# Two transformer blocks on one core: low-order keys beside zeros in 128-row tiles, and value products over 128 columns

## The chip, the cores and the metric

The program runs on one core of one Trainium2 chip. The metric is device time in microseconds of one execution, start to end; of the kernel before there are three timed runs and one further execution that was profiled.

## The reference, cut to what matters

Two transformer blocks run one after the other on a sequence of 1024 tokens of width 1024. The first block holds a differential attention (4 heads, each with two score maps over 64 columns and values 128 wide), a stick-breaking attention (8 heads of 64), a cross attention and an MLP. The second block holds a sliding-window attention (8 query heads over 2 key and value heads of 64, window 128), an RWKV mixer and a gated linear attention (GLA). The change touches three of them:

```python
# differential attention: per head, two maps c over 64 columns each
s = einsum('bhcqd,bhckd->bhcqk', qblk, kh) * scale
p = softmax(where(mask, s, -inf)); w = p[:, :, 0] - lam * p[:, :, 1]
o = einsum('bhqk,bhkv->bhqv', w, vh)
# stick breaking: 8 heads of 64
z = einsum('bhqd,bhkd->bhqk', qblk, kh) * scale
a = exp(where(strict, log_beta + between, -inf)); o = einsum('bhqk,bhkd->bhqd', a, vh)
# sliding window: 8 query heads, 2 key/value heads, blocks of 128
s = einsum('bnqhgd,bnkhd->bnhgqk', qb, kb) * (D ** -0.5) - slopes * dist
p = softmax(concat([where(valid, s, -inf), sink]))[..., :-1]
o = einsum('bnhgqk,bnkhd->bnqhgd', p, vb)      # then gated by silu of another projection
```

## The kernel before, in words

**Precision.** Every large product is done with operands split in two: a high part in float32r and a low part that holds the rest. A projection adds three products (`mm3`, lines 206 to 210: high by high, high by low, low by high). In the attentions the two parts share one tile: `stack_q` (line 434) puts the high part of a head's 64 query rows in one half of the 128 partitions and the low part in the other; `stack_k` (446) puts the high part of the head's keys in both halves of a tile `ks`, so one product over 128 rows gives high by high plus low by high. The low parts of both heads' keys go into one tile `kl`, head 0 in partitions 0 to 63 and head 1 in 64 to 127. The third product is then taken over the 64 rows of one head: line 467 in `scores`, line 1675 in the window attention. On TensorE every score tile is thus a product over 128 rows (466, 1674) followed by one over 64 rows into the same accumulator.

**Values.** In the stick-breaking attention (`sb_units`, 524) the values of a pair of heads lie side by side as 128 columns. Step c of a unit (line 552) multiplies one head's 64 columns into the 64 output partitions of that head (559); both heads of a query block share one PSUM tile, and after head 1 ScalarE copies the whole tile out (564). In the window attention step `pv` (1712) multiplies 64 value columns of group g into 64 partitions (1718); after group 1 VectorE multiplies the tile by the gate (1722). The differential attention has values of 128 columns already (697).

**Order of the work.** The first stage (`mix`, 755) goes through four pairs of stick-breaking heads and then four differential heads. For each, a list of units (query block i, head h) has steps: a (scores and the elementwise chain), b (transposes, 480, copied out at 482), c (value product), and for the differential heads every fourth unit d. `g_units` (725) runs step a of unit k, then b of unit k-2, then c of unit k-4 (lags `LAG`, set at line 801). `weave` (142) fills in projection matmuls of the heads to come between the steps, in proportion to costs written out by hand: `(a, 107 * n), (b, 109 * n), (c, 130 * n)` at line 569, and ratios at lines 814 and 816. Each engine then works through its own queue in order. The stick-breaking chain of step a is: ScalarE sigmoid (539), GpSimd mask (540), VectorE scan (544) and difference (547); then TensorE transposes (480). That of the differential attention: VectorE maximum (663), ScalarE exponential (673), VectorE weighting (684).

The window attention (`w_units`, 1652) runs twice, for tokens 0 to 511 (c = 0) and 512 to 1023 (c = 1), with 8 units each (4 query blocks b by 2 groups g) and lags 0, 2 and 3. Its fill is projection work of the second block. In step `tr` of group 1 the gate rows `sg` are fetched by a DMA on SyncE's queue (1698 to 1702), into a scratch tile of the ring "t2" (5 buffers).

**Memory.** Rings of buffers per tag stand in `BUFS` (187): `kl` has 4 buffers, `wv` 5. Weight pieces go round `wh` (8) and `wv` (`wpiece`, 278): eight pieces hold one set of weights. The rotary step of the differential projection (`g_df_proj`, 609) has four small tiles of its own (627).

Of the kernel before, what the change touches and what calls it, by code (L numbers as in the profile page):

```python
# [22 lines left out]
P = 128  # L23
# [145 lines left out]
class K:  # L169
# [11 lines left out]
    def nm(s, p):  # L181
# [2 lines left out]


    BUFS = {
        "act": 4, "qs": 8, "ks": 8, "kl": 4, "wv": 5, "stg": 3, "pw": 5, "tr": 5, "t2": 5, "v": 3, "u": 1, "wh": 8, "ad": 3, "wt4": 8, 
    }

    def tl(s, pool, shape, tag, dt=F32):  # L190
# [73 lines left out]
    def consts_b(s):  # L264
        nc, A = s.nc, s.A
        c = s.cst
        s.ident = c.tile([P, P], F32, name="ident")
        s.nc.sync.dma_start(s.ident, A["c_id"])
        s.identb = c.tile([P, P], BF16, name="identb")
        nc.vector.tensor_copy(s.identb, s.ident)  # L270
        zb = c.tile([P, P], BF16, name="zb")
        nc.vector.memset(zb, 0.0)
        s.causb = c.tile([P, P], BF16, name="causb")
        nc.gpsimd.affine_select(
            s.causb, zb, pattern=[[-1, P]], compare_op=ALU.is_ge, fill=NEG, base=0, channel_multiplier=1
        )
# [167 lines left out]
        return out  # L444

    def stack_k(s, pool, src, dst=None):
        nc = s.nc
        kl = s.tl(pool, [P, CH], "kl", F32R) if dst is None else dst[2]
        out = []
        for h in range(2):  # L450
            k = s.tl(pool, [P, CH], "ks", F32R) if dst is None else dst[h]
            a, b = slice(64 * h, 64 * h + 64), slice(64 - 64 * h, 128 - 64 * h)
            nc.scalar.activation(k[a], src[a], AF.Copy)
            nc.scalar.activation(k[b], src[a], AF.Copy)
            nc.vector.tensor_tensor(kl[a], src[a], k[a].bitcast(F32), ALU.subtract)
            out.append(k)
        return out + [kl]

    def scores(s, qs, ks, h, i, w0, w1, diag):

        mm = s.nc.tensor.matmul
        c, n = w0 // CH, w1 - w0
        ps = s.ps()
        a = slice(64 * h, 64 * h + 64)
        q = qs[i // 4][h][:, (i % 4) * P : (i % 4 + 1) * P]
        mm(ps[:, :n], q, ks[c][h][:, :n], start=True, stop=False)
        mm(ps[:, :n], q[a], ks[c][2][a, :n], start=False, stop=not diag)
        if diag:
            mm(ps[:, n - P : n], s.identb, s.causb, start=False, stop=True)
        return ps[:, :n]  # L470
# [53 lines left out]
    def sb_units(s, p, res, v):  # L524
        nc = s.nc
        V = nc.vector
        st = {}

        def unit(i, h):
            w = (i + 1) * P  # L530
            u = {}

            def a():
                m = u["m"] = s.tl(s.wk, [P, T + 1], "pw")
                nc.gpsimd.memset(m[:, w : w + 1], 1.0)
                for w0 in range(0, w, CH):
                    w1 = min(w, w0 + CH)
                    ps = s.scores(res["q"], res["k"], h, i, w0, w1, False)
                    nc.scalar.activation(m[:, w0:w1], ps, AF.Sigmoid, scale=s.r18n[:, i : i + 1])
                nc.gpsimd.affine_select(  # L540
                    m[:, w - P : w], m[:, w - P : w], pattern=[[-1, P]], compare_op=ALU.is_gt, fill=1.0,
                    base=0, channel_multiplier=1,
                )
                V.tensor_tensor_scan(  # L544
                    m[:, :w][:, ::-1], m[:, :w][:, ::-1], s.zero.to_broadcast([P, w]), 1.0, ALU.mult, ALU.add
                )
                V.tensor_tensor(m[:, :w], m[:, 1 : w + 1], m[:, :w], ALU.subtract)

            def b():
                u["t"] = s.transposed(u["m"], i + 1)  # L550

            def c():
                if h == 0:
                    st["po"] = s.ps()
                    if i % 4 == 0:
                        st["y"] = s.tl(s.wk, [P, CH], "t2")
                po, y = st["po"], st["y"]
                for j in range(i + 1):
                    nc.tensor.matmul(
                        po[64 * h : 64 * h + 64, :P], v[:, j, 64 * h : 64 * h + 64], u["t"][j],  # L560
                        start=j == 0, stop=j == i,
                    )
                if h == 1:
                    nc.scalar.activation(y[:, (i % 4) * P : (i % 4 + 1) * P], po[:, :P], AF.Copy)
                    if i % 4 == 3:
                        s.put_y(4 + p, i // 4, y)
# [42 lines left out]
    def g_df_proj(s, at, w, res):  # L609
        nc = s.nc  # L610
        V = nc.vector
        wh, wl = w
        for c in range(2):
            u = s.tl(at, [P, 4, 256], "u")
            for b in range(4):
                blk = c * 4 + b
                ps = s.ps()
                yield from s.g_proj_T(blk, wh, wl, 256, ps[:, :256])
                while b == 0 and s.pend:
                    yield from s.pend.pop(0)()  # L620
                nc.scalar.activation(u[:, b, :], ps[:, :256], AF.Copy, scale=s.r1[:, blk : blk + 1])
            uv = u.rearrange("p b (c d) -> p b c d", d=64)
            x1, x2 = uv[:, :, :, 0:8], uv[:, :, :, 8:16]
            sh = [P, 4, 4, 8]
            co = s.cos[:, c * 4 : c * 4 + 4, None, :].to_broadcast(sh)
            si = s.sin[:, c * 4 : c * 4 + 4, None, :].to_broadcast(sh)
            t = [s.sm.tile(sh, F32, tag=f"rt{z}", name=s.nm("rt"), bufs=1) for z in range(4)]
            V.tensor_tensor(t[0], x1, co, ALU.mult)
            V.tensor_tensor(t[1], x2, si, ALU.mult)
            V.tensor_tensor(t[2], x2, co, ALU.mult)  # L630
            V.tensor_tensor(t[3], x1, si, ALU.mult)
            V.tensor_tensor(x1, t[0], t[1], ALU.subtract)
# [960 lines left out]
    def win_load(s, mx, c):  # L1593
# [4 lines left out]
        kst = [mx.tile([P, P + CH], F32R, name=s.nm("k2")) for _ in range(3)]  # L1598
# [53 lines left out]
    def w_units(s, wn, c, qst, kst, bias, sink, one):  # L1652
# [6 lines left out]
        def unit(b, g):  # L1659
# [7 lines left out]
            def a():  # L1667
                p = u["p"] = wn.tile([P, 4, 2 * P], F32, tag="wp", name=s.nm("wp"), bufs=3)
                t = s.sm.tile([P, 6, 4], F32, tag="wt", name=s.nm("wt"))
                for z in range(2):  # L1670
                    ps = s.ps([P, 2, 2 * P])
                    for y in range(2):
                        q = qst[2 * z + y][g][:, (b % 4) * P : (b % 4 + 1) * P]
                        mm(ps[:, y, :w], q, kst[g][:, k0 : k0 + w], start=True, stop=False)  # L1674
                        mm(ps[:, y, :w], q[ga], kst[2][ga, k0 : k0 + w], start=False, stop=True)  # L1675
# [19 lines left out]

            def tr():
                u["t"] = []
                if g == 1:
                    sg = st[("sg", b)] = s.tl(s.wk, [P, 4, P], "t2")
                    s.nc.sync.dma_start(  # L1700
                        sg, s.pd[0:512, b * P : (b + 1) * P].rearrange("(h p) t -> p h t", p=P)
# [8 lines left out]
                    u["t"].append(t)  # L1710

            def pv():
                if g == 0:
                    st["po"] = s.ps()
                po = st["po"]
                for z in range(nk):
                    v = s.vt[:, b - nk + 1 + z, 256 + 64 * g : 320 + 64 * g]
                    mm(po[ga, :], v, u["t"][z], start=z == 0, stop=z == nk - 1)  # L1718
                if g == 1:
                    sg = st.pop(("sg", b))  # L1720
                    y = s.tl(s.wk, [P, 4, P], "t2")
                    V.scalar_tensor_tensor(
                        y, po.rearrange("p (h t) -> p h t", t=P), 0.5, sg, ALU.mult, ALU.mult
                    )
# [681 lines left out]
```

## Time and profile before

| | |
|---|---|
| timed runs | 2459.67, 2461.28, 2468.86 us; median 2461.28 |
| profiled execution | 2454.21 us, its span 2452.0 us |
| granted TensorE clock, mean | 0.973 |
| TensorE matmuls | 12720, busy 95% of the span |
| VectorE, ScalarE, GpSimd busy | 53%, 42%, 28% |

The profile gives for each instruction its engine, line, tile, shape, start and duration. Shapes of a matmul are written as rows*columns of the array, then the size of the moving operand: `64*128 64x512` uses 64 rows and 128 columns and streams 512 columns. The end of a matmul is modelled and matmuls overlap, so its duration is not its price; the price is read from the distance between the starts of neighbours in a view of the instructions in order of time. Such a view merges neighbours of one line into one row with a count, and times are in microseconds from the start of the span.

### The profile page before, as it was taken

The page shows a single profiled execution, that of the slowest core. Times are in us where ns is not written, and L with a number is a line of the kernel's source. Part 1 is how long each engine was busy: PE and PEld are TensorE (multiplying, and loading weights), DVE is VectorE, ACT ScalarE, POOL GpSimd, SP SyncE. Part 2 cuts the span into 40 slices and gives each one's busy share as a digit, 9 for nine tenths or more (in the row PEclk, how much of TensorE's full clock was granted, in tenths as well). Part 3 has the DMA queues.
Part 4 walks back from the last instruction along what each step waited for, and adds up shares of the span by engine and source line. Part 5 has one row for each costly group of instructions (what it writes and reads, how often), then busy time and mean ns, then how long its engine had stood idle before and what let it go on. Part 6 is the DMA issues. An engine that isn't in the chain of part 4 may idle for free. (4 is left out here: it accounts for less than half of the span.)

```text
span 2452.0 us, 34094 instructions
## 1 busy us (share of the span) xinstructions
PE 2339.4 (95%) x12720; PEld 1895.0 (77%) x12720; DVE 1305.7 (53%) x2294; ACT 1032.7 (42%) x2164; POOL 698.4 (28%) x1025
## 2 busy tenths in 40 slices
PE   8999999999999999999999999999998888987996
PEld 7777788887788888888888888887787665676755
DVE  6654555657584465332332332346854666566674
ACT  6554446565463344321321321344533436444363
POOL 3100100000040002355666660025322433224442
PEclk9999999999999999999999999999999899999998
DMA  4010000103232121122222221133332323434361
GB/s 133 27 37 24 22 27 22 44 27 108 82 111 96 62 85 44 56 80 76 76 84 71 80 73 48 52 125 119 128 104 96 122 74 99 144 119 141 112 198 35
DMA packets 116389, 200.01 MB, mean 82 GB/s; under 512 B 14048, under 2 KB 33792, under 8 KB 115456
## 3 DMA queue, kind: packets, MB, share of 16 engines
q1 hardware_dynamic: 111456, 184.72, 23.0%
q0 software_dynamic: 4768, 13.11, 1.7%
q8 instruction: 100, 1.64, 0.3%
q14 instruction: 65, 0.53, 0.1%
HBM read 163.70 MB, written 34.08 MB: 81 GB/s over the span
## 5 line engine op out<-in xcount | busy, mean ns | idle before, releaser
L208 PE MATMUL ps<-act,wh 128*128 128x512 f32 x1680 | 671.9, 402 | 8.1 <-ACT wh L200 5.8
L210 PE MATMUL ps<-act,wh 128*128 128x512 f32 x1656 | 652.8, 394 | 0.6 <-POOL wh L201 0.6
L209 PE MATMUL ps<-act,wh 128*128 128x512 f32 x1496 | 588.4, 394 | 0.5 <-DVE act L204 0.5
L200 ACT ACTIVATE wh<-stg 128x512 fp32r<-128x512 f32 x372 | 233.6, 630 | 603.5 <-PE ps L209 487.5
L208 PEld LDWEIGHTS ps<-act,wh 128*128 128x128 f32 x1680 | 319.4, 190 | 82.9 <-issue 6.9
L210 PEld LDWEIGHTS ps<-act,wh 128*128 128x128 f32 x1656 | 314.5, 190 | 68.2 <-POOL wh L201 1.0
L209 PEld LDWEIGHTS ps<-act,wh 128*128 128x128 f32 x1496 | 283.7, 190 | 58.6 <-issue 1.8
L201 DVE TENSOR_TENSOR wh<-stg,wh 128x512 fp32r<-128x512 f32 x254 | 194.2, 766 | 165.7 <-ACT wh L200 151.2
L201 POOL TENSOR_TENSOR wh<-stg,wh 128x512 fp32r<-128x512 f32 x114 | 159.3, 1401 | 332.9 <-ACT wh L200 301.3
L905 DVE TENSOR_TENSOR act<-ps,act 128x512 f32<-128x512 f32 x112 | 77.0, 689 | 177.4 <-PE ps L210 177.2
L544 DVE TENSOR_TENSOR_SCAN pw<-pw,zero 128x128 f32<-128x128 f32 (+7 forms) x64 | 86.8, 1358 | 103.9 <-POOL pw L540 102.2
L942 POOL TENSOR_TENSOR ad<-ad,cb 128x256 f32<-128x256 f32 x96 | 74.8, 780 | 139.3 <-DMA ad<-adaT 136.4
L1142 DVE SCALAR_TENSOR_TENSOR t<-ps,Rm 128x512 f32<-128x512 f32 x64 | 44.1, 691 | 128.3 <-PE ps L210 127.6
L247 POOL TENSOR_TENSOR nacc<-nacc,t 128x512 f32<-128x512 f32 x28 | 38.2, 1364 | 260.2 <-ACT t L246 255.7
L947 POOL TENSOR_TENSOR ad<-ad 128x128 f32<-128x128 f32 (+5 forms) x288 | 98.6, 342 | 16.8
L208 PE MATMUL ps<-hid,wh 128*128 128x512 f32 x256 | 101.2, 395 | 0.0
L210 PE MATMUL ps<-hid,wh 128*128 128x512 f32 x256 | 101.1, 395 | 0.0
L209 PE MATMUL ps<-hid,wh 128*128 128x512 f32 x256 | 101.0, 394 | 0.0
L1143 ACT ACTIVATE t<-t 128x512 f32<-128x512 f32 x64 | 40.4, 631 | 135.8 <-DVE t L1142 135.8
L482 ACT ACTIVATE tr<-ps 128x512 f32<-128x512 f32 (+3 forms) x144 | 65.8, 489 | 74.0 <-PE ps L480 73.6
L218 POOL TENSOR_TENSOR or<-rsq,mhalf 128x4 f32<-128x4 f32 x8 | 9.7, 1210 | 270.3 <-DVE rsq L217 216.4
L209 PE MATMUL ps<-wh,act 128*128 128x256 f32 x304 | 86.4, 284 | 0.0
(515 smaller groups left out, 4802.9 us busy)
## 6 DMA issues: line engine op xcount, KB each, us to landing
stg<-w2f SPq DMA_DIRECT2D x84, 256.0 KB, 2.9
stg<-w_dn SPq DMA_DIRECT2D x80, 256.0 KB, 2.7
stg<-w_up SPq DMA_DIRECT2D x64, 256.0 KB, 2.6
ad<-adaT POOLq DMA_DIRECT2D x96, 128.0 KB, 2.6
stg<-w2o SPq DMA_DIRECT2D x32, 256.0 KB, 3.2
pd<-t SPq DMA_DIRECT2D x30, 256.0 KB, 2.3
t<-yd SPq DMA_DIRECT2D x26, 256.0 KB, 3.5
rkd<-RK SPq DMA_DIRECT2D x4, 1280.0 KB, 4.5
```

The lines of the kernel that those rows point to most:

```text
L200: nc.scalar.activation(hi, src, AF.Copy)
L201: (eng or nc.vector).tensor_tensor(lo, src, hi.bitcast(F32), ALU.subtract)
L208: mm(out, lh, rh, start=first, stop=False)
L209: mm(out, lh, rl, start=False, stop=False)
L210: mm(out, ll, rh, start=False, stop=last)
L482: nc.scalar.activation(t[:, : m * P], ps[:, : m * P], AF.Copy)
L544: V.tensor_tensor_scan(m[:, :w][:, ::-1], m[:, :w][:, ::-1], s.zero.to_broadcast([P, w]), 1.0, ALU.mult, ALU.add)
L905: s.nc.vector.tensor_tensor(hh, ps, hh, ALU.add)
L942: tt(t, t, cb[:, 256 * y : 256 * y + 256], ALU.mult)
L947: tt(acc[:, n, z, :] if w == 2 else a, a, b, ALU.add)
L1142: V.scalar_tensor_tensor(t, ps, 0.0, R[:, c * CH : (c + 1) * CH], ALU.max, ALU.mult)
L1143: nc.scalar.activation(t, t, AF.Square)
```

## The change: what it does

1. `stack_k` makes two tiles `kl`, one per head: the head's low keys in its own 64 partitions, zeros (a memset on GpSimd) in the other 64. It returns four tiles in place of three; the ring `kl` grows from 4 to 8 buffers, and the window attention's `kst` from 3 to 4 tiles.
2. `scores` and the window's step a take the second product over all 128 rows, with the same query operand as the first; the rows that held nothing of this head meet zeros.
3. Step c of the stick-breaking units multiplies all 128 value columns into 128 partitions, each head into its own 128 columns of the shared PSUM tile, and ScalarE copies the head's own 64 partitions out after each head, so twice per query block and not once.
4. `pv` of the window attention takes a PSUM tile per group, multiplies all 128 value columns, and VectorE gates each group's 64 partitions on its own, in place in `sg`, so twice per query block. The DMA of `sg` is issued in the step `tr` of group 0, one unit earlier; the tile `y` goes.
5. To make room: `wv` has 4 buffers and not 5, the four rotary temporaries become one tile of the ring "t2", and the constant `zb` is taken from "t2".

```diff
-        "kl": 4, "wv": 5,
+        "kl": 8, "wv": 4,
...
-        kl = s.tl(pool, [P, CH], "kl", F32R) if dst is None else dst[2]
         for h in range(2):
             k = s.tl(pool, [P, CH], "ks", F32R) if dst is None else dst[h]
+            kl = s.tl(pool, [P, CH], "kl", F32R) if dst is None else dst[2 + h]
             a, b = slice(64 * h, 64 * h + 64), slice(64 - 64 * h, 128 - 64 * h)
+            nc.gpsimd.memset(kl[b].bitcast(F32), 0.0)
...
-        mm(ps[:, :n], q[a], ks[c][2][a, :n], start=False, stop=not diag)
+        mm(ps[:, :n], q, ks[c][2 + h][:, :n], start=False, stop=not diag)
...
-                        po[64 * h : 64 * h + 64, :P], v[:, j, 64 * h : 64 * h + 64], u["t"][j],
-                        start=j == 0, stop=j == i,
+                        po[:, h * P : (h + 1) * P], v[:, j, :], u["t"][j], start=j == 0, stop=j == i,
...
-                if h == 1:
-                    nc.scalar.activation(y[:, (i % 4) * P : (i % 4 + 1) * P], po[:, :P], AF.Copy)
+                a = slice(64 * h, 64 * h + 64)
+                nc.scalar.activation(y[a, (i % 4) * P : (i % 4 + 1) * P], po[a, h * P : (h + 1) * P], AF.Copy)
...
-            t = [s.sm.tile(sh, F32, tag=f"rt{z}", name=s.nm("rt"), bufs=1) for z in range(4)]
+            t = s.tl(s.wk, [P, 4, *sh[1:]], "t2")
...
-                        mm(ps[:, y, :w], q[ga], kst[2][ga, k0 : k0 + w], start=False, stop=True)
+                        mm(ps[:, y, :w], q, kst[2 + g][:, k0 : k0 + w], start=False, stop=True)
...
-                if g == 1:
+                if g == 0:
                     sg = st[("sg", b)] = s.tl(s.wk, [P, 4, P], "t2")
...
-                    v = s.vt[:, b - nk + 1 + z, 256 + 64 * g : 320 + 64 * g]
-                    mm(po[ga, :], v, u["t"][z], start=z == 0, stop=z == nk - 1)
+                    mm(po, s.vt[:, b - nk + 1 + z, 256:384], u["t"][z], start=z == 0, stop=z == nk - 1)
+                sg = y = st[("sg", b)]
+                V.scalar_tensor_tensor(
+                    y[ga], po[ga].rearrange("p (h t) -> p h t", t=P), 0.5, sg[ga], ALU.mult, ALU.mult
+                )
```

More of the change, by code (lines that the diff above doesn't have):

```diff
@@ L186 @@
     BUFS = {
-        "act": 4, "qs": 8, "ks": 8, "kl": 4, "wv": 5, "stg": 3, "pw": 5, "tr": 5, "t2": 5, "v": 3, "u": 1, "wh": 8, "ad": 3, "wt4": 8,
+        "act": 4, "qs": 8, "ks": 8, "kl": 8, "wv": 4, "stg": 3, "pw": 5, "tr": 5, "t2": 5, "v": 3, "u": 1, "wh": 8, "ad": 3, "wt4": 8,
     }
@@ L270, in consts_b @@
         nc.vector.tensor_copy(s.identb, s.ident)
-        zb = c.tile([P, P], BF16, name="zb")
+        zb = s.tl(s.wk, [P, P], "t2", BF16)
         nc.vector.memset(zb, 0.0)
@@ L447, in stack_k @@
         nc = s.nc
-        kl = s.tl(pool, [P, CH], "kl", F32R) if dst is None else dst[2]
-        out = []
+        out, los = [], []
         for h in range(2):
             k = s.tl(pool, [P, CH], "ks", F32R) if dst is None else dst[h]
+            kl = s.tl(pool, [P, CH], "kl", F32R) if dst is None else dst[2 + h]
             a, b = slice(64 * h, 64 * h + 64), slice(64 - 64 * h, 128 - 64 * h)
+            nc.gpsimd.memset(kl[b].bitcast(F32), 0.0)
             nc.scalar.activation(k[a], src[a], AF.Copy)
@@ L456, in stack_k @@
             out.append(k)
-        return out + [kl]
+            los.append(kl)
+        return out + los
     def scores(s, qs, ks, h, i, w0, w1, diag):
@@ L463, in scores @@
         ps = s.ps()
-        a = slice(64 * h, 64 * h + 64)
         q = qs[i // 4][h][:, (i % 4) * P : (i % 4 + 1) * P]
         mm(ps[:, :n], q, ks[c][h][:, :n], start=True, stop=False)
-        mm(ps[:, :n], q[a], ks[c][2][a, :n], start=False, stop=not diag)
+        mm(ps[:, :n], q, ks[c][2 + h][:, :n], start=False, stop=not diag)
         if diag:
@@ L559, in c @@
                     nc.tensor.matmul(
-                        po[64 * h : 64 * h + 64, :P], v[:, j, 64 * h : 64 * h + 64], u["t"][j],
-                        start=j == 0, stop=j == i,
-                    )
-                if h == 1:
-                    nc.scalar.activation(y[:, (i % 4) * P : (i % 4 + 1) * P], po[:, :P], AF.Copy)
-                    if i % 4 == 3:
-                        s.put_y(4 + p, i // 4, y)
+                        po[:, h * P : (h + 1) * P], v[:, j, :], u["t"][j], start=j == 0, stop=j == i,
+                    )
+                a = slice(64 * h, 64 * h + 64)
+                nc.scalar.activation(y[a, (i % 4) * P : (i % 4 + 1) * P], po[a, h * P : (h + 1) * P], AF.Copy)
+                if h == 1 and i % 4 == 3:
+                    s.put_y(4 + p, i // 4, y)
             n = i + 1
@@ L626, in g_df_proj @@
             si = s.sin[:, c * 4 : c * 4 + 4, None, :].to_broadcast(sh)
-            t = [s.sm.tile(sh, F32, tag=f"rt{z}", name=s.nm("rt"), bufs=1) for z in range(4)]
+            t = s.tl(s.wk, [P, 4, *sh[1:]], "t2")
+            t = [t[:, z] for z in range(4)]
             V.tensor_tensor(t[0], x1, co, ALU.mult)
@@ L1597, in win_load @@
         s.nc.sync.dma_start(sink, s.A["sink"])
-        kst = [mx.tile([P, P + CH], F32R, name=s.nm("k2")) for _ in range(3)]
+        kst = [mx.tile([P, P + CH], F32R, name=s.nm("k2")) for _ in range(4)]
         q8 = s.tl(s.xp, [P, KT, CH], "act", F32R)
@@ L1712, in pv @@
             def pv():
-                if g == 0:
-                    st["po"] = s.ps()
-                po = st["po"]
+                po = s.ps()
                 for z in range(nk):
-                    v = s.vt[:, b - nk + 1 + z, 256 + 64 * g : 320 + 64 * g]
-                    mm(po[ga, :], v, u["t"][z], start=z == 0, stop=z == nk - 1)
-                if g == 1:
[L1720 to L1724, printed above, removed]
+                    mm(po, s.vt[:, b - nk + 1 + z, 256:384], u["t"][z], start=z == 0, stop=z == nk - 1)
[3 more added lines that the diff above has]
+                )
+                if g == 1:
+                    del st[("sg", b)]
                     if c == 1:
```

## The prediction, on record before the changed kernel ran

> **What bounds the kernel now.** I read the page first: its span and busy times.
>
> ```profile
> span 2452.0 us, 34094 instructions
> PE 2339.4 (95%) x12720; PEld 1895.0 (77%) x12720; DVE 1305.7 (53%) x2294; ACT 1032.7 (42%) x2164; POOL 698.4 (28%) x1025
> ```
>
> TensorE is busy for 95% of the span, VectorE for half. Since that busy time is modelled, I next asked for the stretches that the change touches: the stick-breaking units (72 to 400), the differential units (400 to 640) and the two window attentions (2008 to 2072 and 2322 to 2385, followed by their ends).
>
> ```profile
> 72.00:400.00 328.00, 323.84 (x1998) 256.47 (x1998) 181.42 (x216) 163.82 (x349) 26.67 (x120) 0.98 0.08 26
> 400.00:640.00 240.00, 238.04 (x1533) 194.58 (x1532) 152.35 (x376) 138.83 (x408) 8.67 (x7) 1.00 0.17 57
> 2008.00:2072.00 64.00, 64.00 (x262) 42.87 (x261) 47.16 (x108) 39.48 (x98) 20.55 (x17) 1.00 0.33 105
> 2322.00:2385.00 63.00, 60.39 (x250) 39.22 (x249) 51.14 (x88) 37.07 (x98) 29.34 (x21) 1.00 0.60 192
> ```
>
> After the length of the stretch stand PE, PEld, DVE, ACT and POOL busy. TensorE fills all four; VectorE has 45% free in the first, 37% in the second, but only 26% and 19% in the two windows. The waits of TensorE between 60 and 640 say the same: its longest total is
>
> ```profile
> PE ps L480 <- DVE pw L547: 4.2, 5, 1.1
> ```
>
> so in 580 us it stands still for about 6 us. In this stage time is what TensorE's instruction stream costs. The price of that stream I took from starts in the view in order of time.
>
> **What a 64-row product costs.** First neighbours of one array size, 512 columns streamed:
>
> ```profile
> 119.04 0.39 PE L210 MATMUL ps<-act,wh 128*128 128x512 f32 x1
> 119.27 0.39 PE L208 MATMUL ps<-act,wh 128*128 128x512 f32 x1
> ```
>
> One such product costs 0.23. Then two score tiles, each a 128-row and a 64-row product of 512 columns (466, 467, 466, 467), and behind them two projection products:
>
> ```profile
> 208.46 0.39 PE L466 MATMUL ps<-ks,qs 128*128 128x512 f32 x1
> ...
> 210.29 0.28 PE L209 MATMUL ps<-wh,act 128*128 128x256 f32 x1
> ```
>
> From 208.46 to 210.29 are 1.83 us; the last interval holds the first of the projection products, 256 wide, which costs 0.12 otherwise (462.89 to 463.01 below), so the four took 1.71. At 0.23 each they would take 0.92. The surplus is 0.79, or 0.39 per pair: the operands stream at the same rate, so it is paid for going to the other array size and back. With 128 columns:
>
> ```profile
> 132.04 0.22 PE L466 MATMUL ps<-ks,qs 128*128 128x128 f32 x1
> 132.19 0.33 PE L467 MATMUL ps<-kl,qs 64*128 64x128 f32 x1
> ...
> 132.79 0.40 PE L209 MATMUL ps<-act,wh 128*128 128x512 f32 x1
> ```
>
> From 132.04 to 132.79 are 0.75, less 0.23 for the projection product between: 0.52. Two 128-wide products of full size cost 0.11 each (next fence), so the surplus is 0.30. The value product, 64 columns of the array against the 128 of the differential attention:
>
> ```profile
> 396.95 0.28 PE L210 MATMUL ps<-wh,act 128*128 128x256 f32 x1
> 397.16 1.96 PE L559 MATMUL ps<-tr,v 128*64 128x128 f32 x16
> ...
> 399.27 0.28 PE L209 MATMUL ps<-wh,act 128*128 128x256 f32 x1
> ```
>
> ```profile
> 462.89 0.28 PE L210 MATMUL ps<-wh,act 128*128 128x256 f32 x1
> 463.01 1.95 PE L697 MATMUL ps<-v,tr 128*128 128x128 f32 x16
> ...
> 464.91 0.28 PE L209 MATMUL ps<-wv,act 128*128 128x256 f32 x1
> ```
>
> Each stretch has two 256-wide products beside the run of 16 (0.24). So 16 products over 64 columns cost 2.32 - 0.24 = 2.08, and over 128 columns 2.02 - 0.24 = 1.78 (0.11 each). Widening is free and the run loses 0.30. In the window attention a pair of 256 columns:
>
> ```profile
> 2037.11 0.39 PE L1674 MATMUL ps<-k,act 128*128 128x256 f32 x1
> ...
> 2037.74 0.39 PE L1674 MATMUL ps<-k,act 128*128 128x256 f32 x1
> ```
>
> takes 0.63 against 2 x 0.12: surplus 0.39.
>
> **The sum on TensorE.** The counts:
>
> ```profile
> L467 PE MATMUL ps<-kl,qs x192: 322/490/792, 65.5 to 635.4; 64*128 64x512 f32 x96, 64*128 64x128 f32 x32, 64*128 64x256 f32 x32, 64*128 64x384 f32 x32
> L559 PE MATMUL ps<-tr,v 128*64 128x128 f32 x576 | 74.5, 283 | 0.0
> L1675 PE MATMUL ps<-k,act x64: 322/382/579, 2011.6 to 2391.7; 64*128 64x256 f32 x56, 64*128 64x128 f32 x8
> ```
>
> Scores of the first stage: 160 wide pairs x 0.39 = 62.4, and 32 narrow x 0.30 = 9.6. Stick-breaking values: the 576 products stand in 64 runs (4 pairs of heads x 8 blocks x 2), x 0.30 = 19.2. Together 91.2. Window: 56 x 0.39 = 21.8, 8 x 0.30 = 2.4, and 16 value runs at the same 0.30 (nearest row: the run above) = 4.8; together 29.0. All of it is 120.2 us that TensorE's queue no longer spends.
>
> **What of it comes back in the first stage.** Between a unit's last score product and its first transpose there are now 2 to 3 pairs and 1 to 2 value runs, so this time shrinks by 1.1 to 1.8 us in the stick-breaking units, by 1.2 to 1.9 in the differential ones; the chain that must fit into it does not shrink. A tight place:
>
> ```profile
> 239.72 0.43 PE L467 MATMUL ps<-kl,qs 64*128 64x384 f32 x1
> 242.67 0.56 DVE L547 TENSOR_TENSOR pw<-pw 128x384 f32<-128x384 f32 x1
> 243.29 0.55 PE L480 MATMUL ps<-ident,pw 128*128 128x128 f32 x3 [0.33 <-DVE pw L547]
> ```
>
> The chain takes 242.67 + 0.56 - 239.72 = 3.51 and TensorE already waits for it. Between lie the way back from the unit's own 64-row product, one further pair and two value runs: without their surplus it arrives 0.4 + 0.4 + 2 x 0.3 = 1.4 earlier and waits so much longer. I went through the 64 stick-breaking units in this way, from the first (65.5) to the last (376.4), this being the 37th: 12 come out short, by 9.3 in sum. Of the 32 differential units (383 to 635) 4 come out short, by 3.6; the rest keep several microseconds. What is late next is thus VectorE's scan chain, mostly in the short query blocks. Its queue gets denser (181.42 in some 275 us rather than 328), for which I add 4: an estimate. First stage: 91.2 - 17 = 74.
>
> **And in the window.** Of the 29.0, some 24 lie in the two stretches of 127 us in all, where VectorE has 98.3 to do. The gate product now runs twice on half the partitions; its duration follows the elements per partition and stays (0.69):
>
> ```profile
> L1722 DVE SCALAR_TENSOR_TENSOR t<-ps,t x8: 676/692/692, 2046.3 to 2410.9; 128x512 f32<-128x512 f32 x8
> ```
>
> 8 x 0.69 = 5.5 more. So with TensorE at 127 - 24 = 103, VectorE would need about 103 as well, without a gap. Ends: 29 if VectorE's work always fits, 0 if its chains already set the pace. I take the middle, 14; TensorE's full rows speak for the upper half, VectorE's sum for the lower.
>
> **Edits that I cost at nothing.** The 38 memsets lie between a tiny memset of the trace (0.10, 128x1) and a GpSimd pass over 128x512:
>
> ```profile
> L535 POOL MEMSET pw<- x64: 89/99/101, 26.6 to 352.2; 128x1 f32 x64
> L201 POOL TENSOR_TENSOR wh<-stg,wh 128x512 fp32r<-128x512 f32 x114 | 159.3, 1401 | 332.9 <-ACT wh L200 301.3
> ```
>
> that is 4 to 53 us on GpSimd, nearest to the lower end in kind and to the upper in size. 32 of them fall in the first stage, where it has 26.67 of 328 and 8.67 of 240 to do; a mask (540) queued behind one comes at most 1.4 late, four times per head pair. Without that cover it would be 32 x 1.4 = 45. Each waits for a buffer of `kl` two heads old, long read. ScalarE copies twice per block:
>
> ```profile
> L564 ACT ACTIVATE t<-ps x32: 254/278/281, 73.8 to 399.2; 128x128 f32<-128x128 f32 x32
>   PE ps L559: 31.1, 25
> ```
>
> 32 x 0.28 = 9 on an engine with half its time free; it mostly stands there waiting for TensorE. The gate DMA goes ahead of one unit's weight loads on SyncE's queue and holds one scratch tile longer, but only one where there were two. `wv` at 4 leaves half a piece less of weights ahead; pieces are cast after the last projection of a set, whose buffers are free by then. The rotary tile and `zb` take a free slot of "t2"; if none is free, VectorE waits until a copy ends, below 1 us eight times.
>
> **Sum.** 74 + 14 = 88. The profiled execution took 2454.21 (span 2452.0), 7 below the median of the runs, 2461.28. So 2454 - 88 = 2366 under the profiler, and 2461 - 88 = 2373 for the median.
>
> **One rule against it.** Weight loads take 137 ns over 64 columns and 192 over 128:
>
> ```profile
> L559 PEld LDWEIGHTS ps<-tr,v x576: 132/137/230, 72.5 to 398.7; 128*64 128x64 f32 x192
> L697 PEld LDWEIGHTS ps<-v,tr x288: 186/192/246, 403.9 to 655.2; 128*128 128x128 f32 x144
> ```
>
> If loads set the pace of the value runs, widening gives back 576 x 0.055 = 32 us, and the sum is 56: 2405. The two runs of 16 speak against it, since the narrow one is no faster. The Trainium skill, "TensorE: Matmul & The Clock Gate", section "LDWEIGHTS (loading the stationary operand)", says that a load takes its column count over 1.2 in ns and that rows do not matter. By its figures that would be 53 ns more each, an estimate of 31 us, which this trace does not bear out.
>
> **The rivals.**
> - *TensorE's time is all kept*: VectorE's slack absorbs the chains; 88 to 91 in the first stage and 24 of 29 in the window, 113 in all: 2348. For it: chains at most units have 2 us and more to spare.
> - *The chains take half*: with TensorE's stream denser, scan and maximum of neighbouring units queue behind each other, and the window gives nothing: 50 to 55 remain, 2408. For it: VectorE's 51.14 of 63. The rule of wide loads ends nearly there.
> - *Slower*: the two heads' values now share a PSUM tile that ScalarE reads between them. If the tile is guarded as a whole, head 1's first value product waits for head 0's copy, and behind it on TensorE stand the next units' scores and all the fill. This decides from 120.2/32 = 3.8 us per block; at 4.5 it is 144 lost, 24 slower: 2485. Against it: ScalarE waits there for TensorE (31.1 over 25 blocks), and a whole unit lies between the heads.
> - *It does not do what it says*: the surplus comes from the second product reading or accumulating, not from the array size. Then nothing goes, and the copies and gates add little: 2463. Against it: projections accumulate in the same way at 0.23, and the value runs lose the same 0.30 with no second product.
>
> **Chances.** The forecast 0.60, all kept 0.16, half taken 0.14 and wide loads 0.02, slower 0.04, no effect 0.04. The range 2343 to 2413 holds the first four but for their outer edges, and is set by 0 to 29 in the window and by half or none of the chains in the first stage. Half a per cent, 12 us, is about what a measurement of this kernel can tell from no change. Faster 0.92, same 0.04, slower 0.04.
>
> **What would show it.** Right: all rows of 466, 467, 1674 and 1675 read 128*128 and follow at 0.23 for 512 columns; runs of 559 at 0.11; the stage that ended at 640 ends near 566; waits of 480 for 547 rise from 4 to about 15; the window shrinks by 7 each. Wrong: surpluses left at the pairs, waits of TensorE for line 564 or for weight pieces, or VectorE over 90% in the first stage.

## The result and the profile after

| | before | after |
|---|---|---|
| timed runs, median | 2462.70 us (four, 2459.67 to 2468.86) | 2384.23 us (2375.97, 2383.16, 2385.31, and 5296.99) |
| profiled execution | 2454.21, span 2452.0 | 2375.97, span 2374.2 |
| granted clock, mean | 0.973 | 0.973 |

After is 0.9667 of before, 95% interval 0.9633 to 0.9702: faster, by 82.0 us of the means that the ratio compares (2463.5 and 2381.5), by 78.5 us of the two medians, and by 77.8 us of the two profiled spans, which had the same clock. The run of 5297 us was disturbed; it counts in the median of after and is left out of the ratio.

The page of after first: its span and busy times.

```profile
span 2374.2 us, 34207 instructions
PE 2239.0 (94%) x12720; PEld 1891.3 (80%) x12720; DVE 1308.5 (55%) x2302; ACT 1035.1 (44%) x2196; POOL 710.2 (30%) x1063
```

As many products, 100 us less of TensorE's busy time; the other engines did 2 to 12 us more. Next the stretches that answer to those of before, with PE, PEld, DVE, ACT and POOL busy behind the length, then the granted clock, the DMA share and GB/s: stick-breaking, differential, and the two windows.

```profile
72.00:353.00 281.00, 275.35 (x1993) 256.84 (x1992) 179.45 (x215) 166.47 (x382) 34.67 (x136) 0.99 0.09 30
353.00:568.00 215.00, 209.05 (x1523) 190.60 (x1523) 148.44 (x375) 137.05 (x402) 12.05 (x15) 0.99 0.19 63
1937.00:2000.00 63.00, 58.09 (x270) 42.03 (x268) 51.52 (x117) 43.07 (x111) 20.30 (x17) 1.00 0.35 116
2246.00:2305.00 59.00, 52.05 (x250) 40.51 (x248) 47.71 (x80) 35.84 (x93) 29.21 (x22) 0.94 0.61 201
```

The same work stands in 281 us instead of 328 and in 215 instead of 240. TensorE has more gaps than before: 5.7 and 6.0 us are free in the first two (4.2 and 2.0 before), 4.9 and 7.0 in the windows (none and 2.6 before). VectorE went to 64%, 69%, 82% and 81%. Now the products themselves, in order of time: two score tiles (512 and 384 columns), and a run of 16 value products between its neighbours.

```profile
104.72 0.40 PE L468 MATMUL ps<-ks,qs 128*128 128x512 f32 x1
104.95 0.40 PE L469 MATMUL ps<-kl,qs 128*128 128x512 f32 x1
105.19 0.33 PE L468 MATMUL ps<-ks,qs 128*128 128x384 f32 x1
105.36 0.34 PE L469 MATMUL ps<-kl,qs 128*128 128x384 f32 x1
105.53 0.40 PE L210 MATMUL ps<-act,wv 128*128 128x512 f32 x1
...
345.42 0.28 PE L210 MATMUL ps<-wv,act 128*128 128x256 f32 x1
345.54 1.95 PE L561 MATMUL ps<-tr,v 128*128 128x128 f32 x16
347.24 0.37 PE L208 MATMUL ps<-wv,act 128*128 128x256 f32 x1
347.44 0.28 PE L209 MATMUL ps<-wv,act 128*128 128x256 f32 x1
```

All rows read 128*128. A score pair of 512 columns takes 0.47 where it took some 0.85. The 16 value products start 1.70 apart from what follows, and the whole from 345.42 to 347.44 is 2.02, where the same sequence took 2.32 before. The zeros cost TensorE nothing.

To put the gain in places I read start times from both traces. The **score stretch** runs from the first to the last score product's start. Its **surplus** is its length less what all its matmuls cost at the steady distances of neighbours of one size (0.229, 0.174, 0.120 and 0.110 us for 512, 384, 256 and 128 columns; with unrounded distances 479.9 in all, within 0.2 the same for every kernel). The surplus falls into what stands at **changes of array size** and what stands at **gaps** between products of one size. Of the **stage end** (last transposes of the differential heads) I give the start.

| | before | after | difference |
|---|---|---|---|
| score stretch | 65.4 to 635.4 | 66.2 to 566.9 | -69.3 |
| of it at changes of size | 80.8 (477 places) | 0 | -80.8 |
| of it gaps at one size | 9.4 | 20.8 | +11.4 |
| stage end | 665.0 | 594.5 | -70.5 |
| first window, length | 93.7 | 86.5 | -7.2 |
| second window, length | 87.5 | 79.9 | -7.6 |

This division is rough in two ways: a few waits of before stand at changes of size (the transposes at 74.1 and 75.9 us waited 1.0 and 0.8), and the distance behind a change is longer too, which counts as a gap (more on this with the scores alone).

The gain of 70.5 stays whole until the first window begins (2011.5 became 1940.7). Each window keeps 5 more at the point that follows it, 10.1 in all. The two lengths shrank by more, 14.8 together, because projection products now stand behind the last value product, where they no longer count in the length (2027.27 to 2029.98 in after, 2.7 us). Between the windows 2.8 go back, where RWKV transposes wait for a DMA (4.4 in place of 3.0). At the end 77.8 are left. The views of TensorE's waits, first stage and second window of after:

```profile
PE ps L482 <- DVE pw L549: 3.6, 5, 1.0
PE ps L641 <- DVE u L635: 2.6, 1, 2.6
PE ps L712 <- ACT t L707: 1.9, 1, 1.9
PE ps L561 <- ACT t L565: 1.9, 4, 0.6
```

```profile
PE ps L1718 <- ACT act L1711: 6.6, 5, 2.4
PE ps L1708 <- ACT wp L1693: 5.9, 3, 2.3
```

Columns: total, times, longest. The second window had 3.7 and 2.4 of these two before; the first had 6.2 for ScalarE's scaling of the weights (`wp`) and has 8.9 now.

### The profile page after: what moved, and what is told of

Read it like the earlier page. It is cut to its first block, busy times and chain, and to the rows that moved or that the text cites. A ratio compares the mean times of both kernels' runs of the same rounds, so it can differ in the third digit from the quotient of the medians.

```text
span 2374.2 us, 34207 instructions
## 1 busy us (share of the span) xinstructions
PE 2239.0 (94%) x12720; PEld 1891.3 (80%) x12720; DVE 1308.5 (55%) x2302; ACT 1035.1 (44%) x2196; POOL 710.2 (30%) x1063
## 4 chain that ended last, share of the span: by engine, by line
PE 76%; DVE 12%; DMA 4%; ACT 4%; issue 4%; POOL 1%; SPq 0%; DVEq 0%; ACTq 0%; POOLq 0%
PE ps L208 20%; PE ps L209 20%; PE ps L210 20%; PE ps L561 3%; PE ps L482 2%; PE ps L469 1%; PE ps L468 1%; PE ps L699 1%; DVE act L1944 1%; DVE itmp L1941 1%; PE ps L1820 1%; PE ps L1718 1%; DMA stg<-w_xv 1%; ACT pw L675 1%; DVE gqd L2101 1%
## 5 line engine op out<-in xcount | busy, mean ns | idle before, releaser
L208 PE MATMUL ps<-wh,act 128*128 128x256 f32 x320 | 95.6, 299 | 0.0
L210 PE MATMUL ps<-wh,act 128*128 128x256 f32 x320 | 91.0, 284 | 0.0
L209 PE MATMUL ps<-wh,act 128*128 128x256 f32 x320 | 90.7, 284 | 0.0
```

What stands on the lines that cost most here:

```text
L208: mm(out, lh, rh, start=first, stop=False)
L209: mm(out, lh, rl, start=False, stop=False)
L210: mm(out, ll, rh, start=False, stop=last)
```

## The experiments

Each kernel was run beside the kernel before. Single profiled spans differ by up to 1% with the granted clock (0.963 to 0.973), so I read the surplus and the stage end beside the ratios. Most of this difference lies between the two windows: from the last value product of the first to the first score product of the second the twelve profiles take 217 to 234 us.

| kernel | median us | ratio to before (95%) | changes | surplus | stage end |
|---|---|---|---|---|---|
| before | 2462.70 | 1 | 477 | 90.1 | 665.0 |
| after | 2384.23 | 0.9667 (0.9633 to 0.9702) | 0 | 20.8 | 594.5 |
| values at 64 columns | 2395.70 | 0.9734 (0.9692 to 0.9776) | 116 | 37.4 | 609.3 |
| window as before | 2386.84 | 0.9696 (0.9657 to 0.9735) | 0 | 23.2 | 596.6 |
| before, grouped | 2441.19 | 0.9915 (0.9881 to 0.9948) | 375 | 71.6 | 645.9 |
| PSUM tile per head | 2376.21 | 0.9652 (0.9622 to 0.9682) | 0 | 21.3 | 594.3 |
| more fill early | 2391.78 | 0.9702 (0.9662 to 0.9742) | 0 | 27.7 | 599.9 |
| zeros written once | 2378.45 | 0.9666 (0.9638 to 0.9693) | 0 | 20.7 | 593.1 |
| less fill in the window | 2390.64 | 0.9701 (0.9669 to 0.9732) | 0 | 21.3 | 596.1 |
| scores over 64 rows | 2448.26 | 0.9927 (0.9898 to 0.9956) | 383 | 88.5 | 664.0 |
| window, longer lag | 2372.22 | 0.9631 (0.9605 to 0.9656) | 0 | 20.8 | 594.1 |
| preparation alone | 2465.83 | 1.0030 (1.0016 to 1.0044) | 477 | 92.7 | 668.7 |

My theory going in: the gain is the price of going to another array size and back. Rivals: what the second product reads, the load of wide weights, the shared PSUM tile.

**Values back at 64 columns** (after, with the old step c):

```diff
-                        po[:, h * P : (h + 1) * P], v[:, j, :], u["t"][j], start=j == 0, stop=j == i,
+                        po[64 * h : 64 * h + 64, :P], v[:, j, 64 * h : 64 * h + 64], u["t"][j],
```

> The changed kernel with one part undone: the stick-breaking value products take 64 columns again, both heads in one tile and one copy per block. Theory (each going to another array size and back costs TensorE about 0.3 us, and the first stage is bound by TensorE): 64 runs x 0.30 = 19 us come back on TensorE, some 2 to 4 of it into waits that it has now; the stage's end moves from 594.5 to about 611, the whole is 15 to 19 slower than the changed kernel, near 2392 by profile. Rival (the gain is all in the scores, the value runs were paced by their weight loads or hidden): within 4 of the changed kernel.

The stage ends at 609.3, 14.8 later, and the surplus rose by 16.6 for 116 changes. A run of 16 in its order of time:

```profile
358.50 0.28 PE L210 MATMUL ps<-wv,act 128*128 128x256 f32 x1
358.71 1.96 PE L561 MATMUL ps<-tr,v 128*64 128x128 f32 x16
360.60 0.39 PE L208 MATMUL ps<-wh,act 128*128 128x256 f32 x1
360.82 0.28 PE L209 MATMUL ps<-wh,act 128*128 128x256 f32 x1
```

Against after: 0.21 instead of 0.12 into the run, 1.89 instead of 1.70 to what follows, 0.22 instead of 0.20 behind it; together 0.30, at the two ends and not per product. That rules wide loads out as the pace: 16 products over 128 columns are no slower than over 64. The Trainium skill, "TensorEngine Tiling (Array Packing)", section "Key Properties", says that changing the tiling mode drains the engine. The trace shows a price at such a change, here 0.30 there and back for columns; that a drain is what it pays for is not shown.

**The window as before** (after, with the old window attention and its three key tiles):

```diff
-                        mm(ps[:, y, :w], q, kst[2 + g][:, k0 : k0 + w], start=False, stop=True)
+                        mm(ps[:, y, :w], q[ga], kst[2][ga, k0 : k0 + w], start=False, stop=True)
...
-                    mm(po, s.vt[:, b - nk + 1 + z, 256:384], u["t"][z], start=z == 0, stop=z == nk - 1)
+                    mm(po[ga, :], v, u["t"][z], start=z == 0, stop=z == nk - 1)
```

> The changed kernel with the window attention as it was before (three key tiles, 64-row second products, 64 value columns, one gate per block). Reading of the two profiles: the window's two runs gained 5.0 and 5.1 us, of which 2.8 was given back at the loads of the next RWKV stage; so this run is 7 slower than the changed kernel, near 2383 by profile, and the first stage's end stays at 594.5. The prediction's term would make it 14 slower (2390); a window bound by its chains alone would make it 0 to 2.

Windows of 94.3 and 87.3, and from stage end to the end of the span 1789.7 against 1779.7 of after: the window's part is worth 7 to 10 (part of the 10 is the lower clock of this run, 0.968 against 0.973). It is real, and smaller than the 14 of the prediction. The ratios alone (0.9696 and 0.9667) do not tell the two kernels apart.

**Before, with products of one size grouped.** Everything as before, but each unit writes all its 128-row score products first and then all its 64-row ones:

```diff
-        mm(ps[:, :n], q, ks[c][h][:, :n], start=True, stop=False)
-        mm(ps[:, :n], q[a], ks[c][2][a, :n], start=False, stop=not diag)
+        for ps, (h, w0, w1, diag) in zip(out, parts):
+            mm(ps[:, : w1 - w0], q(h), ks[w0 // CH][h][:, : w1 - w0], start=True, stop=False)
+        for ps, (h, w0, w1, diag) in zip(out, parts):
+            a = slice(64 * h, 64 * h + 64)
+            mm(ps[:, : w1 - w0], q(h)[a], ks[w0 // CH][2][a, : w1 - w0], start=False, stop=not diag)
```

> The kernel before, with no product changed: of each unit of the two attentions of the first stage, all 128-row score products are issued first, then all 64-row ones. 96 of the 192 pairs of size changes in the scores go (32 in the stick-breaking units, 64 in the differential ones). Theory (the price hangs on the change of size): 96 x 0.38 = 36 us less on TensorE, less 3 to 8 that chains which start later give back: the first stage ends at 632 to 638 and not 665, the whole 28 to 33 faster than the kernel before, near 2424 by profile. Rival (the price is that of the 64-row product itself, or of its load): no gain, 0 to 5 slower.

The 192 products over 64 rows are all there, on the same operands; only neighbours changed. In the queue the groups were split: 91 of these products still stand alone, 90 in 45 pairs, the rest in three runs of 3 and 4. Changes fell by 102 and the surplus by 18.5, 0.18 per change; the stage ended 19.1 earlier and the kernel is 0.5 to 1.2% faster. Less than I expected since only half of the groups held, but it settles that the price hangs on the change of size, not on the product.

**Scores alone back over 64 rows** (after, values and window as changed):

```diff
-        mm(ps[:, :n], q, ks[c][2 + h][:, :n], start=False, stop=not diag)
+        a = slice(64 * h, 64 * h + 64)
+        mm(ps[:, :n], q[a], ks[c][2 + h][a, :n], start=False, stop=not diag)
```

> The changed kernel, with only the second score product of the first stage taken over the head's own 64 rows again (the zeros stay, the value products stay at 128 columns, the window stays changed). Theory, a price of about 0.146 us for each change of array size: some 360 to 384 changes come back among the score products, the surplus over the steady price goes from 20.8 to 73 to 77 us, and the end of the first stage from 594.5 to 647 to 651, since the value products alone gave back 14.8 of 70.5. The profiled span is then 2427 to 2431, 1.2 to 1.4% below the kernel before. Rival, changes of the row count cost more than changes of the column count (0.18 each, the slope between the kernel before and the one with grouped score products): the surplus is 86 to 90 and the stage ends at 660 to 664, hardly before that of the kernel before.

The rival's figures hold, 88.5 and 664.0; a price of 0.146 for every change is wrong, and the price of a pair that the prediction had read is near right. The median over the 192 places is 0.176 into 64 rows and 0.194 out, 0.37 per pair. Into and out of 64 columns the medians are 0.090 and 0.093 on top of the steady price. Two tiles of 384 columns in the order of time show a pair:

```profile
388.31 0.42 PE L468 MATMUL ps<-ks,qs 128*128 128x384 f32 x1
388.67 0.44 PE L470 MATMUL ps<-kl,qs 64*128 64x384 f32 x1
389.04 0.23 PE L472 MATMUL ps<-causb,identb 128*128 128x128 bf16 x1
389.08 0.42 PE L468 MATMUL ps<-ks,qs 128*128 128x384 f32 x1
```

From one product to the next 0.36 and 0.37, where 0.174 is the steady distance. So most of the stage's gain hangs on the scores.

The rival's reason, that rows cost more than columns, does not follow from these medians, since the places differ. A change lengthens two distances, the one at it and the next. Where two full-size products of 256 columns or more stand ahead, the way into 64 rows costs 0.09 in the kernel before (36 places) and into 64 columns also 0.09 (35). The next distance is longer by 0.10 where its product streams 256 columns or more, behind 64 rows (43 places) as behind 64 columns (36), and by 0.05 where it streams 128. A lone 64-row product has the second half of the way in on its way out, hence 0.194; and its way in often follows another change, or a 128-column product behind which the next one starts early. Where two 64-row products stand together, in the grouped kernel, the way out is 0.09 (42 places):

```profile
114.75 0.71 PE L466 MATMUL ps<-ks,qs 128*128 128x512 f32 x2
115.39 0.73 PE L470 MATMUL ps<-kl,qs 64*128 64x512 f32 x2
116.05 0.50 PE L208 MATMUL ps<-act,wh 128*128 128x512 f32 x1
116.39 0.40 PE L209 MATMUL ps<-act,wh 128*128 128x512 f32 x1
```

The two take 0.66 where 0.46 is steady: the second half of the way in and the first of the way out. The product behind them takes 0.34 in place of 0.23. So a change costs some 0.19 beside long products and 0.14 where the next one streams 128 columns, as in the value runs, for rows and columns alike.

Left alone, the value products should still have gained their 11.6 of changes; but this kernel's gaps are 20.0, 10.6 more than before's. Some of that is the clock. The stretch from 80 to 100 us of this kernel, and the same of before (the third figure from the end is the granted clock):

```profile
80.00:100.00 20.00, 19.64 (x74) 14.59 (x73) 7.19 (x8) 6.63 (x14) 1.87 (x8) 0.65 0.00 0
```

```profile
80.00:100.00 20.00, 20.00 (x93) 14.11 (x93) 11.27 (x12) 9.04 (x18) 2.02 (x10) 0.86 0.04 14
```

74 products instead of 93 were done there, at 0.65 instead of 0.86; 0.21 of 20 us is 4.2. Corrected by that the stage ends near 660, at the rival's edge. By the clock records of the whole stage (mean 0.977 against 0.987) it is some 7, and the end near 657, between theory and rival. Three further gaps, 2.75, 1.98 and 1.18, lie in the differential part. Timed runs of the same clock are the better comparison: 2437.5 against 2459.6 and 2460.1 at 0.970, 22 us, which is about the window's 7 to 10 and the values' 11.6. After and before differ by 78 at 0.973 in the same way, so the scores' share is some 56.

**The preparation alone.** Gaps of the same size stand in after (2.76, 2.02 and 1.18, the middle one at another product), so I asked whether they belong to the shorter stream of TensorE at all. This kernel has every product of before and only the padded key tiles, the memsets and the changes of buffers:

```diff
-        "kl": 4, "wv": 5,
+        "kl": 8, "wv": 4,
...
+            nc.gpsimd.memset(kl[b].bitcast(F32), 0.0)
...
-            t = [s.sm.tile(sh, F32, tag=f"rt{z}", name=s.nm("rt"), bufs=1) for z in range(4)]
+            t = s.tl(s.wk, [P, 4, *sh[1:]], "t2")
```

> Every matrix product as in the kernel before (64-row second score products, 64-column stick-breaking values, the window attention as it was); of the change only the preparation is left: two zero-padded key tiles per pair of heads with their 32 memsets on GpSimd, eight buffers for them, weight ring of 4 and not 5, rotary temporaries and the constant in the ring t2. The theory on record says that the preparation costs nothing and that the gaps between products of one size (9.4 us in the score stretch before, 20.8 after) came because TensorE's stream got shorter: with the stream as long as before, gaps of 8 to 11, the surplus at 88 to 92, the end of the stage at 664 to 667, and the time within 5 us of the kernel before. Rival, the preparation itself costs some 11 us (the kernel with 64-row scores and wide values had gaps of 20.0 although its stream was as long as before): gaps of 18 to 22, the surplus at 99 to 103, the stage ends at 674 to 678, and the time is 8 to 14 us above that of the kernel before.

It lies between the two, nearer to the theory in the stage: gaps of 12.3 against 9.4, surplus 92.7, stage end 668.7 (3.7 later, 2.4 of it from a later start of the score stretch). In time it is 0.16 to 0.44% slower, 7.8 us by the medians. Only the 3.7 are shown to be the preparation's. Of the 13.5 by which its profiled span is longer, 11.0 lie between the two windows, where the same 1290 matmuls ran at a lower granted clock (third figure from the end), in before and here:

```profile
2105.00:2323.00 218.00, 189.71 (x1290) 150.38 (x1288) 140.40 (x238) 86.91 (x164) 81.32 (x64) 0.92 0.38 123
2108.00:2337.00 229.00, 202.79 (x1290) 161.54 (x1288) 142.31 (x238) 86.08 (x164) 81.28 (x64) 0.87 0.36 119
```

Its timed runs had clocks of 0.965 to 0.968, most of those of before beside them a higher one (0.964 to 0.973). At 0.967 five runs of it took 2464.1 to 2467.6, and six of before, from all experiments, 2460.9 to 2469.9. Whether the preparation has a part in the lower clock is not shown. Its waits of TensorE:

```profile
PE ps L656 <- DVE u L650: 4.4, 2, 2.6
PE ps L496 <- DVE pw L563: 4.4, 5, 1.1
```

The first row is new: before has no wait of these transposes in this stage. They wait for the rotary step of the differential projection. In after, the view of VectorE in order of time shows what is late:

```profile
386.29 0.28 DVE L633 TENSOR_TENSOR t<-u,sin 128x128 f32<-128x128 f32 x1
386.49 0.74 DVE L714 TENSOR_SCALAR t<-ps,gsub 128x512 f32<-128x512 f32 x1
387.15 0.34 DVE L700 TENSOR_SCALAR t<-ps,rc 128x128 f32<-128x128 f32 x1
387.41 0.68 DVE L201 TENSOR_TENSOR wv<-stg,wv 128x512 fp32r<-128x512 f32 x1
388.01 0.28 DVE L634 TENSOR_TENSOR u<-t 128x128 f32<-128x128 f32 x1
```

Three other passes (1.5 us) stand between the rotary's four products and its two sums. Whether the shared ring or the order of the queue put them there was not separated.

**A PSUM tile per head** (after; the heads no longer share one):

```diff
-                if h == 0:
-                    st["po"] = s.ps()
+                po = s.ps()
...
-                        po[:, h * P : (h + 1) * P], v[:, j, :], u["t"][j], start=j == 0, stop=j == i,
+                        po[:, :P], v[:, j, :], u["t"][j], start=j == 0, stop=j == i,
```

> The changed kernel with a PSUM tile of its own for each head's values, so that head 1's value products need not wait for the copy of head 0. The changed kernel's profile has this wait (TensorE's value product for ScalarE's copy) at 1.9 us, 4 times. Theory (the slower rival's mechanism is there, and small): the wait goes, the whole is 0 to 3 faster than the changed kernel by profile, less than timing can tell. Rival (the shared tile holds TensorE up at more places, under other names): 6 or more faster.

The wait for the copy (1.9 in after) is gone from the list, and the one for VectorE's difference took its place:

```profile
PE ps L482 <- DVE pw L549: 6.6, 5, 1.9
```

The stage ends at 594.3 against 594.5. The rival's mechanism exists, but is worth nothing: in its place the next link of the chain is late.

**More fill beside the early blocks** (after; extra projection work given to the short query blocks):

```diff
-                e0 = (100 if kind == "s" else 370)
-                e1 = (1000 if kind == "s" else 8)
+                e0 = (500 if kind == "s" else 370)
+                e1 = (5 if kind == "s" else 8)
```

> The changed kernel with more projection work beside the short query blocks of the stick-breaking heads (the extra per unit 500 falling to 0 over the first five blocks, and not a constant 100), nothing else. In the changed kernel the score stretch (66.2 to 566.9) holds 20.8 us over the steady price of its matmuls. If what is left are chains that come late at short blocks, 3 to 8 of it goes and the stage ends at 587 to 592. Rival (chains come late at long blocks or at the head change just as often, or the surplus is no wait at all): no change or up to 4 later.

A miss: the stage ends at 599.9, 5.4 later, and the wait for the difference doubled (7.2 against 3.6). The new waits stand some 25 us into a head pair (at 95.24 us TensorE waits 1.5 for the difference, where after waits for nothing): fill given early is missing later, and the hand-tuned order was the better one.

**Zeros written once** (after; eight fixed key tiles, so 8 memsets in the first stage and not 32):

```diff
-            nc.gpsimd.memset(kl[b].bitcast(F32), 0.0)
+            if new:
+                nc.gpsimd.memset(kl[b].bitcast(F32), 0.0)
```

> The changed kernel with eight fixed tiles for the low keys of the first stage, whose zero halves are written once, so 8 memsets of it remain and not 32. In the changed kernel GpSimd waits 56.8 us in 10 memsets for the last reader of a buffer, with the next masks queued behind. Theory (the masks that matter are not behind these waits): the waits go, the whole stays within 3. Rival (late masks are part of the 20.8 us of surplus): 5 or more faster.

Stage end 593.1 against 594.5, the same ratio. The memsets are hidden. In after the group and its wait read

```profile
L454 POOL MEMSET kl<- x32: 518/520/525, 0.7 to 455.3; 64x512 f32 x32
...
  PE ps L469: 56.8, 10
```

GpSimd stands 56.8 us ahead of ten of them waiting for a buffer to be read, and TensorE's waits, the same in both kernels, do not show it.

**Less fill in the window** (after): `(a, -3000)` became `(a, -2300)`.

> The changed kernel with the share of fill beside a window unit cut from 3000 to 2300. The window gained 10 and not 29 us. If that is because the units now come to their chains with the fill used up (TensorE idle at the end of both windows, waiting for ScalarE), spreading the fill makes the window's chains start earlier and the whole 3 to 8 faster. Rival (VectorE and ScalarE set the pace of the units throughout): the units do not come closer, 0 to 3 either way.

A miss too: windows of 87.6 and 84.7 instead of 86.5 and 79.9, the second in part by a lower clock (0.88 against 0.94 in it). TensorE's waits for ScalarE's scaling and copies grew from 9.9 to 11.7 in the first window and from 12.5 to 13.9 in the second.

**A longer lag in the window** (after; transposes and value products one unit later, no buffer added):

```diff
+        s.LAG = (0, 3, 4)
         yield from s.g_units(s.w_units(mx, c, qst, kst, bias, sink, one), tail, first)
         yield from s.g_drain(tail)
+        s.LAG = K.LAG
```

> The changed kernel, with the window attention's transposes and value products one unit later (lags 0, 3, 4 in place of 0, 2, 3; no buffer added). Theory, the window's gain stopped at half because TensorE now waits for the elementwise chain of a unit (waits of the transposes and value products for ScalarE of 8.9 us in the first window and 12.5 in the second): one more unit between them takes away most of the waits inside a window, but the last unit has one unit less of work behind which to hide, so 0 to 6 us faster, with the waits of the second window at 4 to 8 instead of 12.5. Rival, the engines' work itself and not the latency sets the pace of the window: waits as long as before, only for other producers, and 0 to 5 us slower through the longer end.

Windows of 82.9 and 76.8, so 3.6 and 3.1 shorter. The wait for the scaling (8.9 and 5.9) is gone. The value products now wait longer for ScalarE's copies, 6.8 in the first window (1.0 in after), and in the second

```profile
PE ps L1720 <- ACT act L1713: 8.2, 5, 2.6
```

Both together fell from 9.9 to 6.8 and from 12.5 to 8.2, just short of the 4 to 8 expected. That speaks for latency: a unit's chain needs more cover than TensorE's shorter work now gives it. Its ratio is the lowest of all, but its interval overlaps that of after, so I do not call it faster. In the profiled spans nothing of it is left, 1779.7 from the stage end to the end as in after, since the stretch between the windows took 10.5 more at a lower clock (0.87 against 0.92). Timed runs at 0.970 took 2367.0 to 2373.2 here (four), and 2375.6 and 2377.0 with a tile per head and with the zeros written once.

## Why the prediction was right, step by step

**The price per pair** (0.39 wide, 0.30 narrow; 72.0 for 192) stands, near enough. Before's 192 pairs have 69.2 at their changes, 0.36 each; the kernel with the scores alone undone has 68.5. Grouping showed that it hangs on the neighbours.

**The value runs** (64 x 0.30 = 19.2) were oversized in the count. The 0.30 is right for a run between full-size products, and undoing them cost 14.8 to 16.6. But there are 58 runs and not 64, since some units' runs join, and in before 22 of them stand directly behind a 64-row score product and share its change. The changes at values alone hold only 11.6 in that trace, without the longer distances behind them. The two parts are not additive: the 14.8 are what values cost beside full-size scores.

**What comes back in the first stage** (13 for short chains and 4 for a denser VectorE queue, so 17) was too large, and its mechanism was not borne out. The gaps grew by 11.4, and the waits that the profile lists for TensorE in the stretch grew from 6.1 to 11.4. I expected the growth at the transposes that wait for the difference, from 4 to about 15; they went from 4.2 to 3.6. Why the units that I had counted as short kept up stays open. What is new are 2.6 for the rotary step, 1.9 for the copy out of the shared PSUM tile, 1.0 for the low part of a projection's input (201), and 1.3 more at line 712. The first and the third come with the preparation alone, whose list adds up to 10.4. A wait for that copy was among the prediction's signs of being wrong; it is there, but small.

So 91.2 - 17 = 74 became 80.8 - 11.4 = 69.4 in the stretch and 70.5 at the stage end. Both terms were too large, by 10 and by 6, and that the two errors nearly cancel is luck.

**The window** (29.0 off TensorE, 14 kept) was the term that was mis-sized most. The 64 pairs have 0.385 each at their changes by the medians, 25 in all, and the value runs some 0.3 to 0.4 each, so what TensorE was spared is about as forecast. Of it 10.1 were kept in the two windows and 2.8 of these given back at the RWKV transposes: 7.3. The 14 was the middle between two ends and not read from a row. I reasoned with VectorE's sum of work (98 of 127), which would have fitted; the waits that grew are those for ScalarE's scaling and copies in one unit's chain. The longer lag, which shortened the windows by 6.7, speaks for the latency of that chain.

**Edits costed at nothing.** The memsets, the doubled copies and the shared PSUM tile are covered, as forecast. The rotary step was not: I gave it below 1 us eight times, and it is waited for once in after (2.6) and twice with the preparation alone (4.4 in all). That kernel's stage ends 3.7 later; how much of its 4 to 11 us in time is the clock was not separated.

**The rivals.** All kept (2348) and half taken (2408) lie on either side of the 2384 measured; no effect and slower are out, and so are wide loads (2405), by the runs of 16. Summed up: the forecast of 88 against 78 in the profiled spans, short by 3.5 in the first stage and by 7 in the window.

## What to carry to other kernels

Count the places where neighbouring products on TensorE change rows or columns of the array, and read the price of a change from starts in the order of time, the distance behind the change included; where a narrow operand alone among full-size ones can lie beside zeros, or be multiplied with its neighbour at no extra streamed columns, the wider product is the cheaper one. Undoing parts one at a time is needed to divide such a gain, because neighbouring parts share changes. In the window attention part of what was taken from a full engine came back as waits for a chain that it used to cover: the latency of a unit against its lag told more there than the sum of the other engine's work.

## What the runs showed of the hardware that was not expected

In the score stretch a change of array size is paid in two distances: some 0.09 us at the change, and another 0.10 at the next distance (0.05 where that product streams 128 columns), alike for 64 rows and 64 columns. Read at the change alone, 64 rows look twice as dear (0.176 and 0.194 us in and out, against 0.090 and 0.093; medians over 192, 191, 36 and 58 places), because these products stand alone and their neighbours differ. The way out does not depend on the length of a run: it is 0.09 behind runs of 2 and of 16 value products over 64 columns.

The time of one kernel follows the granted clock from run to run: the kernel with 64-row scores took 2427.5 us at 0.977 and 2455.0 at 0.963, before 2451.0 at 0.973 and 2473.2 at 0.963. A difference of 10 us between two single profiles says little unless their clocks agree.
